# A decoder trunk on one core: the opening written out as one list per engine, Silu from Exp and Ln in the gated mixer, heads closed singly, 1/rms on VectorE

## The chip, the cores and the metric

The kernel runs on one core of a Trainium2 chip. The metric is the time of one execution on the device in microseconds (us), as the median of several runs. The engines are named as in the profile: PE is the matrix engine (TensorE) and PEld its weight loads, DVE is VectorE, ACT is ScalarE, POOL is GpSimd, SP is SyncE, whose queue issues most of the transfers. Each engine works through its own list of instructions in order and waits where an operand or a buffer is not ready.

## The reference

The program is a decoder trunk of two layers over 512 tokens of width 1024, all in 32-bit floats. Each layer is a half-step feed-forward block (FFN), a mixer, and a second half-step FFN, each behind an RMSNorm with a learned gain. Layer 0's mixer is gated linear attention (GLA) with 4 heads, layer 1's is stick-breaking attention (SB) with 16. Cut to what this change touches:

```python
def rmsnorm(x, g):
    y = x * lax.rsqrt(jnp.mean(x * x, axis=-1, keepdims=True) + EPS)
    return y * g

def swiglu(h, w_gate, w_up, w_down):          # width 2816 in between
    return (silu(h @ w_gate) * (h @ w_up)) @ w_down

# GLA, after the chunked attention has given o of 4 heads x 256:
    o = rmsnorm(o, o_norm)
    o = o * silu(g)                           # g: 1024 columns of h @ w_in
    return o @ w_out
```

## The kernel before

Activations are kept with features on the 128 partitions: `xs[0..7]` are eight tiles of 128 features by 512 tokens. Every large product is made three times to keep its precision: each operand is cut into a high part (cast on ACT, L133 for weights) and a low part (difference on DVE, L134), and `mm3` issues high x high, low weight x high and high weight x low.

Weights come through `feed`, a list of entries. An entry is a piece of a weight matrix with the products on it; a `feat` entry has eight steps over the input features with three products each, 24 products into one PSUM bank. Starting an entry cuts the weights of the next three and loads those of the next six. The weights' cuts have four buffers, so the cut of an entry waits until PE is done with the entry four before it. The order on each engine within these rules is found by a scheduler that works with costs of its own.

**Opening.** x arrives as eight tiles of 128 tokens by 512 features, four for the left half of the features and four for the right (L1288). PE turns them with transposes (`turn`, L1312), ACT and DVE make the cut `xh`, `xl` of x times the gain straight from PSUM (L1323, L1324), and the first two entries (gate and up weights of the first 128 columns, one transfer of 512 KB each) run on them. At this point 1/rms is not known. So the first entries of an FFN run on x that is not normed, and their results are multiplied by 1/rms on the way out of PSUM: the first two are held back (`defer`) until it is there, the next ones pay one more DVE operation each. Meanwhile `normed_input` makes the normed x (`xn`, L610), its cut `nh`, `nl` (L616, L617) and the sums `ts` that later entries need. `NORMED` = 6 is the entry from which the products run on `nh` and `nl`.

**1/rms.** `stats_a` sums the squares over features and calls `rstd`: a Sqrt on ACT (L384), with the table load that it needs, the reciprocal and a correction on DVE. `stats_b` spreads the four columns over 512 tokens with a product of ones and diagonal tiles (`dg`, `ps_R`) into `R` and `Rq`. This happens at the opening and once ahead of each of the five further blocks.

**GLA.** The feed's entries (queries, keys, values by `tok`, then the eight tiles of the gate g by `feat`, evacuated times R into `gn`, L754) are stepped between the levels of the four heads' attention, each of which has a chain DVE, ACT (Exp of `e`), DVE, PE (`ps_S`). `output(h)` normalizes a head: `vv` on DVE, Ln, Exp and Square on ACT, three DVE operations, then `on`. When the last head's levels are done, `silu` puts all eight `gn` through Silu (L966), the tables of Exp and Ln are loaded again (L434), and heads 0, 1 and 2 are closed: `on` times `gn` (L971), cut into `oh` (L974) and `ol` (L975). Then the output projection (`ps_b`, by `back`) begins, and head 3 is closed inside it.

Of the kernel before, what the change touches and what calls it, by code (L numbers as in the profile page):

```python
# [10 lines left out]
F32 = mybir.dt.float32  # L11
F32R = mybir.dt.float32r
BF16 = mybir.dt.bfloat16
U8 = mybir.dt.uint8
AF = mybir.ActivationFunctionType
# [15 lines left out]
def decoder(ctx: ExitStack, tc: tile.TileContext, a: dict, out: bass.AP):  # L31
# [345 lines left out]
    def rstd(sums, n, more=None):  # L377
# [5 lines left out]
        y = sp.tile([P, n], F32, tag="ry", bufs=2, name="ry")  # L383
        st["sqrt"] = nc.scalar.activation(y, v, AF.Sqrt).ins  # L384
        nc.vector.reciprocal(y, y)
        q = sp.tile([P, n], F32, tag="rq", bufs=2, name="rq")
        if n == 1:
            nc.vector.scalar_tensor_tensor(out=q, in0=y, scalar=v, in1=y, op0=ALU.mult, op1=ALU.mult)
        else:
            nc.vector.tensor_tensor(out=q, in0=y, in1=y, op=ALU.mult)  # L390
            nc.vector.tensor_tensor(out=q, in0=q, in1=v, op=ALU.mult)
        c = float(D) ** 0.5
# [49 lines left out]
    class FFN:  # L442
# [10 lines left out]
        def __init__(self, wg, wu, wd, gi, nxt, first=False, last=False):  # L453
            self.gi, self.normed = gi, False
# [3 lines left out]
            base, downs = len(feed.q), []  # L458
            self.sums_by = 10**6
            for group, (c0, c1) in enumerate(self.GROUPS):  # L460
                slots, put = 2 * (c1 - c0), 0
                for i in range(slots):
# [13 lines left out]
                    elif c not in self.SEVEN_UP:  # L476
                        feat(g, f_, self.evac_g, defer=d, part=3 if len(feed.q) == 0 else KD // 2, o=quads, m=four)
                    elif f == 0:
                        feat(g, 0, self.evac_g, o=quads, m=four), feat(g, 1, self.evac_g, o=quads, m=four)
# [194 lines left out]
        def run(self, between=None):  # L674
            with tc.tile_pool(name="hp", bufs=8, reuse_waits="tile") as self.hp, tc.tile_pool(
# [8 lines left out]
                for job, n in ((self.normed_input, self.NORMED - 2), (self.sums, self.sums_by - self.NORMED)):  # L684
# [16 lines left out]
    class GLA:  # L701
        def __init__(self, w_in, w_gk2, b_gk, og, w_out, nxt):
# [15 lines left out]
            for c in range(4):  # L718
# [33 lines left out]
        def evac_g(self, j, ps):  # L752
# [3 lines left out]
            )  # L756

# [205 lines left out]
        def silu(self):  # L963
            for j in range(KD):
                with tc.issue_after(st["last"]):
                    s = nc.scalar.activation(self.gn[j], self.gn[j], AF.Silu).ins  # L966
            exp_ln_tables(s)

# [9 lines left out]
        def run(self):  # L978
            with ExitStack() as es:
# [7 lines left out]
                new_norm()  # L987
                self.gate_weights()
# [6 lines left out]
                exp_ln_tables(st["sqrt"])  # L995
# [6 lines left out]
                for h in range(4):  # L1002
# [28 lines left out]
    class SB:  # L1031
# [139 lines left out]
        def run(self):  # L1171
            with ExitStack() as es:
# [10 lines left out]
                new_norm()  # L1183
                two_halves()
# [3 lines left out]
                exp_ln_tables(st["sqrt"])  # L1188
# [79 lines left out]
    with tc.tile_pool(name="ip", bufs=1) as ip:  # L1268

        gls = [ip.tile([P, P], F32, name=f"gl{n}") for n in range(2)]  # L1270
        for gl in gls:
            nc.vector.memset(gl, 0.0)
        x0 = {}
        lead = phases[0].lead
# [7 lines left out]

        gains(0, ("ffn1_norm",))
        gains(1, ("mix_norm", "ffn2_norm", "gla_o_norm"))
        for hf in range(2):
            for i in range(NT):
                x0[i, hf] = ip.tile([P, T], F32, name=f"x0_{i}_{hf}")
                nc.sync.dma_start(x0[i, hf], a["x"][0, i * P : (i + 1) * P, hf * T : (hf + 1) * T])  # L1288
            for c in lead[:1] if hf == 0 else lead[1:]:
                c.pool = ip  # L1290
                c.load()
        st["ss"] = None
# [123 lines left out]
```

## Time and profile before

| | |
|---|---|
| runs | 1831.14, 1831.64, 1832.43 us; median 1831.64 |
| profiled execution | 1831.4 us |
| its span, first to last instruction | 1829.6 us, granted clock 0.997 |
| busy PE / PEld / DVE / ACT / POOL | 1794.3 / 1643.0 / 1458.5 / 944.3 / 8.5 us |
| HBM | 175.17 MB read, 97 GB/s over the span |

A row of the profile gives the source line, engine, operation, output and inputs with their shapes. In the order of time it begins with the start and the length in us; a count (x4) says that several were merged. What stands in brackets is the idle time of the engine just before and what ended it. The rows of waits give the waiting instruction, what it waited for, and us in total, times, and the longest. Lengths of neighbouring instructions overlap, since an engine begins the next before the last has drained; how often one comes is read from the starts.

### The profile page before, as it was taken

The numbers are of one execution on the slowest core, as the hardware profiler recorded it, in microseconds if no ns is written. First come the engines' busy times: TensorE is split into PE (matmuls) and PEld (weight loads), VectorE is DVE, ScalarE is ACT, GpSimd is POOL, SyncE is SP. The second block draws the span as 40 slices with busy tenths as digits, with TensorE's granted clock in tenths as the row PEclk, the third lists the DMA queues.
The fourth block names the chain that finished last, engine by engine and source line by source line (L and its number), as shares of the span: only waits on it lengthen the run. The fifth ranks groups of instructions, "written<-read, shape, count | busy, mean of one in ns | idle before, by whom it ended". The sixth has DMA issues, their size and how long they took to land.

```text
span 1829.6 us, 28900 instructions
## 1 busy us (share of the span) xinstructions
PE 1794.3 (98%) x11790; PEld 1643.0 (90%) x11790; DVE 1458.5 (80%) x2317; ACT 944.3 (52%) x1459; POOL 8.5 (0%) x20
## 2 busy tenths in 40 slices
PE   7999999999989999999999999999999999999998
PEld 6899999889978899999989999999888788999997
DVE  5987878775776988887888888787887769888785
ACT  5444444543674644444454444345888844444444
POOL 0000000100000000000000000000000000000000
PEclk9999999999999999999999999999999999999999
DMA  5333332322112333333223333233212133333321
GB/s 162 116 104 104 104 119 90 115 70 70 61 55 71 119 121 111 110 107 103 92 92 127 104 113 115 96 94 101 73 58 70 51 111 115 104 105 104 117 92 69
DMA packets 177576, 179.09 MB, mean 98 GB/s; under 512 B 4066, under 2 KB 167956, under 8 KB 177444
## 3 DMA queue, kind: packets, MB, share of 16 engines
q1 hardware_dynamic: 176192, 175.13, 29.6%
q8 instruction: 92, 1.51, 0.3%
q0 software_dynamic: 576, 1.05, 0.2%
q10 hardware_dynamic: 676, 1.07, 0.2%
q14 instruction: 40, 0.33, 0.1%
HBM read 175.17 MB, written 2.10 MB: 97 GB/s over the span
## 4 chain that ended last, share of the span: by engine, by line
PE 85%; DVE 6%; ACT 4%; DMA 3%; issue 1%; SPq 1%; DVEq 0%; ACTq 0%
PE ps_d L62 23%; PE ps_f L62 15%; PE ps_w L530 14%; PE ps_z L530 9%; PE ps_q L530 9%; PE ps_t L62 4%; PE ps_b L62 3%; DVE wl L134 2%; PE ps_S L62 1%; DMA raw<-in_ffn_w_up_dram 1%; DMA raw<-in_ffn_w_gate_dram 1%; PE ps_bt L62 1%; ACT wh L133 1%; PE ps_oT L1158 1%; PE ps_z L1096 1%
## 5 line engine op out<-in xcount | busy, mean ns | idle before, releaser
L134 DVE TENSOR_TENSOR wl<-raw,wh 128x1024 fp32r<-128x1024 f32 x244 | 261.8, 1073 | 61.9 <-ACT wh L133 61.0
L133 ACT CAST wh<-raw 128x1024 fp32r<-128x1024 f32 x244 | 225.9, 928 | 131.3 <-PE ps_f L62 41.8
L62 PE MATMUL ps_d<-hh,wh 128*128 128x512 f32 x672 | 254.9, 379 | 0.0
L62 PE MATMUL ps_d<-hh,wl 128*128 128x512 f32 x672 | 254.7, 379 | 0.0
L62 PE MATMUL ps_d<-hl,wh 128*128 128x512 f32 x672 | 254.7, 379 | 0.0
L133 ACT CAST wh<-s 128x1024 fp32r<-128x1024 f32 x136 | 142.2, 1046 | 117.1 <-PE ps_q L530 84.1
L134 DVE TENSOR_TENSOR wl<-s,wh 128x1024 fp32r<-128x1024 f32 x136 | 166.1, 1221 | 26.3 <-ACT wh L133 24.9
L62 PE MATMUL ps_f<-xh,wh 128*128 128x512 f32 x448 | 176.6, 394 | 5.3 <-ACT wh L133 3.7
L308 DVE SCALAR_TENSOR_TENSOR x<-ps_d,x 128x512 f32<-128x512 f32 x184 | 125.2, 689 | 61.2 <-PE ps_d L62 61.0
L62 PE MATMUL ps_f<-xh,wl 128*128 128x512 f32 x448 | 171.6, 383 | 0.5 <-DVE wl L134 0.5
L62 PE MATMUL ps_f<-xl,wh 128*128 128x512 f32 x448 | 170.9, 382 | 0.0
L530 PE MATMUL ps_z<-th,wh 128*128 128x256 f32 x544 | 149.9, 276 | 2.4 <-DVE u L541 2.4
L133 ACT CAST wh<-rawd 128x1024 fp32r<-128x1024 f32 x84 | 87.9, 1047 | 121.9 <-PE ps_d L62 103.9
L530 PE MATMUL ps_w<-nh,wl 128*128 128x256 f32 x544 | 149.6, 275 | 0.0
L530 PE MATMUL ps_w<-nl,wh 128*128 128x256 f32 x544 | 149.6, 275 | 0.0
L530 PE MATMUL ps_z<-th,wl 128*128 128x256 f32 x544 | 149.6, 275 | 0.0
L530 PE MATMUL ps_z<-tl,wh 128*128 128x256 f32 x544 | 149.6, 275 | 0.0
L530 PE MATMUL ps_w<-nh,wh 128*128 128x256 f32 x544 | 149.5, 275 | 0.0
L62 PEld LDWEIGHTS ps_d<-hl,wh 128*128 128x128 f32 x672 | 127.0, 189 | 18.0
L62 PEld LDWEIGHTS ps_d<-hh,wl 128*128 128x128 f32 x672 | 127.2, 189 | 16.6
L62 PEld LDWEIGHTS ps_d<-hh,wh 128*128 128x128 f32 x672 | 127.2, 189 | 16.5
L134 DVE TENSOR_TENSOR wl<-rawd,wh 128x1024 fp32r<-128x1024 f32 x84 | 102.8, 1224 | 34.7 <-ACT wh L133 34.3
(260 smaller groups left out, 4719.8 us busy)
## 6 DMA issues: line engine op xcount, KB each, us to landing
raw<-in_ffn_w_gate_dram SPq DMA_DIRECT2D x43, 1024.0 KB, 5.2
raw<-in_ffn_w_up_dram SPq DMA_DIRECT2D x43, 1024.0 KB, 5.2
rawd<-in_ffn_w_down_dram SPq DMA_DIRECT2D x84, 512.0 KB, 3.4
raw<-in_gla_w_in_dram SPq DMA_DIRECT2D x12, 1024.0 KB, 5.2
raw<-in_sb_w_in_dram SPq DMA_DIRECT2D x16, 512.0 KB, 3.7
raw<-in_gla_w_out_dram SPq DMA_DIRECT2D x4, 1024.0 KB, 4.9
raw<-in_sb_w_in_dram SPq DMA_DIRECT2D x4, 1024.0 KB, 5.2
raw<-in_sb_w_out_dram SPq DMA_DIRECT2D x4, 1024.0 KB, 4.8
```

Source lines behind the costliest of these rows:

```text
L62: st["pe"] = nc.tensor.matmul(ps, l, r, start=first, stop=last).ins
L133: nc.scalar.copy(h, r).ins,
L134: nc.vector.tensor_tensor(out=l, in0=r, in1=h.bitcast(F32), op=ALU.subtract).ins,
L308: nc.vector.scalar_tensor_tensor(out=x, in0=back_by(ps, 4), scalar=0.5, in1=x, op0=ALU.mult, op1=ALU.add)
L530: nc.tensor.matmul(pairs(o), l_, r_, start=first and j + n == 0, stop=j == 3 and n == 2, skip_group_check=True)
L1096: nc.tensor.matmul(o_, l_, r_, start=first, stop=last, skip_group_check=True)
L1158: nc.tensor.matmul(po[e * 64 : e * 64 + 64, j * P : T], self.v[j][:, c : c + 64], self.wt[p, e][bk][:, c0 : c0 + n], start=j == 0, stop=j ...
```

## The change

**The opening** is written out in one order (`manual_schedule`). PE begins with eight products of a tile of ones (`filler`, made by a memset on DVE) into a bank that nobody reads, and has eight more between the transposes. x's first half is turned tile by tile instead of feature block by feature block. The weights of the first two entries come in halves: the four steps for the left half of the features first, then x's right half, then the second four; they are also cut in halves (`w_high`, `w_low`). The eight products of the left half for both entries are interleaved with the transposes of x's right half. The gains other than the first are fetched from ACT's queue after its second square. The first FFN's third entry is also held back until 1/rms is known, and `NORMED` is 7 for this FFN.

**1/rms** (`rstd` for four columns): two DVE operations on the bits of v as integers give a first value, three rounds of three DVE operations refine it. ACT has no part in it. The four last ones at the end of the program (one column each) keep the Sqrt. **Tables:** those of Exp and Ln are loaded after the last Silu of the FFN ahead of a mixer instead of after the Sqrt.

**GLA:** `evac_g` makes Silu at once, as g times Exp(min(g, 0) - Ln(1 + Exp(-|g|))): Abs, Exp and Ln on ACT, one DVE operation, Exp on ACT, one DVE product. `silu` is gone. A head is closed when the next head's levels have been worked through (`self.close(h - 1)`). In the feed the two gate tiles of a head follow its value entry.

```diff
+        if n > 1:
+            nc.vector.tensor_scalar(
+                out=q.bitcast(I32), in0=v.bitcast(I32), scalar1=1, scalar2=None, op0=ALU.arith_shift_right
+            )
+            nc.vector.tensor_scalar(
+                out=y.bitcast(I32), in0=q.bitcast(I32), scalar1=-1.0, scalar2=float(0x5F3759DF), op0=ALU.mult, op1=ALU.add
+            )
+            for k in (1.0, 1.0, c):
+                nc.vector.tensor_tensor(out=q, in0=y, in1=y, op=ALU.mult)
+                nc.vector.scalar_tensor_tensor(out=q, in0=q, scalar=-0.5 * k, in1=v, op0=ALU.mult, op1=ALU.mult)
+                nc.vector.scalar_tensor_tensor(out=y, in0=q, scalar=1.5 * k, in1=y, op0=ALU.add, op1=ALU.mult)
+            return y
...
+            if first:
+                self.NORMED = 7
...
+                        feat(g, f_, self.evac_g, defer=self.defer if first and i == 1 else d, o=quads, m=four)
...
-                two_halves(stats_a, 2 - (feed.pos == 1))
-                stats_b(turned=True)
-                flush(self.defer)
+                if self.first:
+                    with tc.manual_schedule():
+                        feed.entries(1)
+                        stats_b(turned=True)
+                        flush(self.defer)
...
             for c in range(4):
                 tok(w_in, 1024 + c * 256, lambda i, ps, c=c: self.evac_v(c, i, ps), "a")
-            for c in range(4):
                 ch = Chunk(cols(w_in, 2048 + c * 256, 256), KD, 256)
...
+            g = self.gn[j]
+            t = self.ep.tile([P, T], F32, tag="sg", bufs=2, name="sg")
+            nc.scalar.activation(t, g, AF.Abs)
+            act(t, t, AF.Exp, scale=-1.0)
+            act(t, t, AF.Ln, bias=1.0)
+            nc.vector.scalar_tensor_tensor(out=t, in0=g, scalar=0.0, in1=t, op0=ALU.min, op1=ALU.subtract)
+            act(t, t, AF.Exp)
+            nc.vector.tensor_tensor(out=g, in0=g, in1=t, op=ALU.mult)
...
-        def silu(self):
-            for j in range(KD):
-                with tc.issue_after(st["last"]):
-                    s = nc.scalar.activation(self.gn[j], self.gn[j], AF.Silu).ins
-            exp_ln_tables(s)
...
+                exp_ln_tables(st["silu"])
-                exp_ln_tables(st["sqrt"])
...
                         for _ in prev:
                             feed.step(1)
+                        self.close(h - 1)
                     prev = self.output(h)
-                    if h == 3:
-                        while feed.pos < self.end:
-                            feed.step(1)
-                        feed.finish()
-                        next(prev)
-                        self.silu()
-                        for g in range(3):
-                            self.close(g)
+                while feed.pos < self.end:
+                    feed.step(1)
+                feed.finish()
...
+        fill(8)
+        square(0, 0)
+        turn(0, 0, range(4))
+        ps = psum("ps_g", "t")
+        nc.tensor.transpose(ps[:, 0:P], gls[0], ident)
+        nc.vector.tensor_copy(gT[:, 0:16], ps[:, 0:16])
+        square(0, 1)
+        turn(0, 1, range(4))
+        fill(3)
+        gains(1, ("mix_norm", "ffn2_norm", "gla_o_norm"))
+        square(0, 2)
+        turn(0, 2, range(4))
+        fill(1)
+        turn(0, 3, range(4))
+        fill(4)
+        high(0), low(0)
+        w_high(0, 0), w_low(0, 0)
+        prod(0, 0)
+        px += [psum("ps_x", t) for t in "tt"]
+        turn(1, 0, (4, 5))
+        high(1), low(1)
+        prod(0, 1)
...
```

In the instructions, the opening changes on PE as follows. Before, from the last transpose of x's left half (`x_3_0`) to the first products (`ps_f`) of the first entry:

```order
L1312 MATMUL ps_x<-ident,x_3_0_105 128x128
L1318 MATMUL ps_g<-ident,gl_91 128x128
L62 MATMUL ps_f<-xh,wh 128x512
L62 MATMUL ps_f<-xh,wl 128x512
L62 MATMUL ps_f<-xl,wh 128x512
```

The same place in the changed kernel:

```order
L1342 MATMUL ps_x<-ident,x_3_0_107 128x128 x4
L63 LDWEIGHTS filler
L63 MATMUL ps_i<-filler 128x512
...
L63 MATMUL ps_f<-xh,wh 128x512
L63 MATMUL ps_f<-xh,wl 128x512
L63 MATMUL ps_f<-xl,wh 128x512
L1342 MATMUL ps_x<-ident,x_0_1_113 128x128 x2
L63 MATMUL ps_f<-xh,wh 128x512
```

The products of a feature block now stand between transposes of x's right half (`x_0_1`), and fillers stand where PE had nothing.

On DVE, from the sum of squares (`rv`) to 1/rms over the tokens (`R`) in the first FFN; `wl` are cuts of weights for later entries, `rq` and `r` the small steps of 1/rms. Before:

```order
L1367 COPY gT<-ps_g 128x34
L1369 TENSOR_TENSOR sums<-sums_123,sums_124 128x4
L380 TENSOR_SCALAR rv<-sums 128x4
L134 TENSOR_TENSOR wl<-raw_121,wh 128x1024
L385 RECIPROCAL ry<-ry 128x4
L134 TENSOR_TENSOR wl<-raw,wh 128x1024
L390 TENSOR_TENSOR rq<-ry 128x4
L134 TENSOR_TENSOR wl<-raw,wh 128x1024
L391 TENSOR_TENSOR rq<-rq,rv 128x4
...
L404 TENSOR_SCALAR dg<-ident,r_303 128x128 x4
L409 COPY R<-ps_R 128x512
```

In the changed kernel:

```order
L1433 COPY gT<-ps_g 128x34
...
L135 TENSOR_TENSOR wl<-raw_125,wh 128x1024
L381 TENSOR_SCALAR rv<-sums 128x4
L135 TENSOR_TENSOR wl<-raw,wh 128x1024
L389 TENSOR_SCALAR rq<-rv 128x4
L135 TENSOR_TENSOR wl<-raw,wh 128x1024
L392 TENSOR_SCALAR r_325<-rq 128x4
...
L397 SCALAR_TENSOR_TENSOR rq<-rq,rv 128x4
L135 TENSOR_TENSOR wl<-raw,wh 128x1024
L398 SCALAR_TENSOR_TENSOR r_325<-rq,r_325 128x4
L414 TENSOR_SCALAR dg<-ident,r_325 128x128 x4
L419 COPY R<-ps_R 128x512
```

A further cut (`wl`) has come in front of the last small step, and the copy of the gains `gT`, which needs a transpose that PE has behind all products of the first two entries, stands ahead of it all.

On ACT, at the end of GLA, where head 2 is finished (`y` are the steps of its norm, `osq` and `sh` its squares) and `oh` is what the output projection needs. Before:

```order
L439 ACT_TABLE_LOAD
L439 ACTIVATE y<-vv 128x512
L439 ACT_TABLE_LOAD
L439 ACTIVATE kd<-kd 128x384
L439 ACTIVATE y<-y 128x512
L966 ACT_TABLE_LOAD
L966 ACTIVATE gn<-gn 128x512
L950 ACTIVATE y_5358<-y 128x512
L966 ACTIVATE gn<-gn 128x512
L434 ACT_TABLE_LOAD
L974 CAST oh<-on 128x512 x4
```

In the changed kernel (`sg` are the steps of the gate's Silu):

```order
L449 ACTIVATE y<-vv 128x512
L779 ACTIVATE sg<-gn 128x512
L449 ACTIVATE y<-y 128x512
L449 ACTIVATE sg<-sg 128x512
L978 ACTIVATE y_5461<-y 128x512
L449 ACTIVATE sg<-sg 128x512
L449 ACTIVATE kd<-kd 128x384
L449 ACTIVATE sg<-sg 128x512
L134 CAST wh<-raw 128x1024
L932 COPY kt<-ps_kd 128x384
L996 CAST oh<-on 128x512 x2
```

The table loads are gone, the gate's four steps stand between those of the norm, and only head 2's two `oh` are left here; those of heads 0 and 1 stand earlier.

More of the change, by code (lines that the diff above doesn't have):

```diff
@@ L14 @@
 U8 = mybir.dt.uint8
+I32 = mybir.dt.int32
 AF = mybir.ActivationFunctionType
@@ L1281, in gains @@
                 row += r.shape[0]
+        filler = ip.tile([P, T], BF16, name="filler")
+        nc.vector.memset(filler, 1.0)
+        for gl in gls:
+            nc.vector.memset(gl, 0.0)
         gains(0, ("ffn1_norm",))
-        gains(1, ("mix_norm", "ffn2_norm", "gla_o_norm"))
[L1285 to L1291, printed above, removed]
@@ L1346, in decoder @@
-        with behind(turned[2]):
-            feed.q[0].split()
-        with behind(st["cut"]):
-            keep(pst, 0)
-        body = feed.q[0].body(feed.q[0].W)
-        next(body)
-        with tc.issue_after(st["pe"]):
-            pst = turn(1)
-        with behind(turned[5]):
-            feed.q[1].split()
-        with behind(turned[7]):
-            keep(pst, 1)
-            feed.start()
-        with behind(st["cut"]):
-            squares(0, (2, 3))
-            squares(1, range(NT))
@@ L1362, in decoder @@
-        for _ in body:
-            pass
-        ps = psum("ps_g")
-        with tc.issue_after(st["pe"]):
-            nc.tensor.transpose(ps[:, 0:P], gls[1], ident)
+        nc.scalar.preload_act_table_set("silu_and_others")
+        for hf in range(2):
+            rows_of(hf)
+            first_weights(hf)
+        for c in lead[2:]:
+            c.pool = ip
+        for en in feed.q[2:8]:
+            for u in en.units:
+                u[0].load()
+        W = []
+        for _ in range(2):
+            W.append(tuple(wp.tile([P, KD, P], F32R, tag="w" + t, bufs=4, name="w" + t) for t in "hl"))
@@ new lines, in decoder, with fill, turn @@
+        px = [psum("ps_x", t) for t in "aazz"]
+        pg, pu = psum("ps_f", "z"), None
+        idle = psum("ps_i", "o")
+        sums = [ip.tile([P, NT], F32, name=f"sums{hf}") for hf in range(2)]
+        nh, nl = [], []
+        def fill(n):
+            for _ in range(n):
+                mm(idle, filler[:, 0:P], filler, True, True)
+        def turn(hf, i, ks):
+            for k in ks:
+                nc.tensor.transpose(
+                    px[k][:, i * P : (i + 1) * P], x0[i, hf][:, (k % 4) * P : (k % 4 + 1) * P], ident
+                )
@@ new lines, in decoder @@
+        fill(1)
[8 more added lines that the diff above has]
+        prod(0, 1)
+        turn(1, 1, (4, 5))
+        high(2), low(2)
+        prod(0, 2)
+        turn(1, 2, (4, 5))
+        high(3), low(3)
+        w_high(1, 0), w_low(1, 0)
+        prod(0, 3)
+        pu = psum("ps_f", "o")
+        prod(1, 0)
+        turn(1, 3, (4, 5))
@@ new lines, in decoder @@
+        keep(0, 1, 2, 3)
+        prod(1, 1)
+        px += [psum("ps_x", t) for t in "aa"]
+        for i in range(NT):
+            turn(1, i, (6, 7))
+        prod(1, 2)
+        square(0, 3)
+        prod(1, 3)
+        w_high(0, 1), w_low(0, 1)
+        for k in range(4, KD):
+            high(k), low(k)
+            prod(0, k)
+        w_high(1, 1), w_low(1, 1)
+        for k in range(4, KD):
+            prod(1, k)
+        f1.defer += [(f1.evac_g_, pg), (f1.evac_u_, pu)]
+        feed.q[2].split()
@@ L1367, in decoder @@
+        for i in range(NT):
+            square(1, i)
+        ps = psum("ps_g", "z")
+        nc.tensor.transpose(ps[:, 0:P], gls[1], ident)
         nc.vector.tensor_copy(gT[:, 16:50], ps[:, 16:50])
+        keep(4, 5, 6, 7)
         st["sums"] = sp.tile([P, NT], F32, tag="rq", bufs=2, name="sums")
         nc.vector.tensor_tensor(out=st["sums"], in0=sums[0], in1=sums[1], op=ALU.add)
+        st["ss"], st["nh"], st["nl"] = None, nh, nl
+        stats_a()
+        turn_[0] = 3
+        feed.pos = 2
```

118 lines of the change are left out of this document (55 added, 63 removed).

## The prediction

> **What bounds the kernel now.** I read the first and fourth part of the page, then the waits of TensorE (PE), the busy times by stretch, and the order of time where PE stands idle.
>
> ```profile
> PE 1794.3 (98%) x11790; PEld 1643.0 (90%) x11790; DVE 1458.5 (80%) x2317; ACT 944.3 (52%) x1459; POOL 8.5 (0%) x20
> PE 85%; DVE 6%; ACT 4%; DMA 3%; issue 1%; SPq 1%; DVEq 0%; ACTq 0%
> ```
> ```profile
> PE ps_R L62 <- DVE dg L404: 1.9, 1, 1.9
> PE ps_f L62 <- DVE wl L134: 2.1, 2, 1.7
> PE ps_S L62 <- DVE e L844: 1.1, 1, 1.1
> ```
> ```profile
> 0.00:10.00 10.00, 4.64 (x17) 3.39 (x17) 0.43 (x4) 2.62 (x5) 0.70 (x6) 1.00 0.75 240
> 10.00:20.00 10.00, 5.98 (x22) 4.62 (x23) 5.22 (x9) 5.08 (x9) 0.00 (x0) 1.00 1.11 322
> 30.00:40.00 10.00, 8.06 (x34) 6.62 (x33) 7.99 (x18) 3.68 (x6) 0.00 (x0) 0.83 0.00 1
> 540.00:550.00 10.00, 5.72 (x20) 4.61 (x21) 8.07 (x13) 8.73 (x13) 0.00 (x0) 0.83 0.00 0
> ```
> PE is busy for 1794.3 of 1829.6 us and its products stay as they are, so the prize is 35.3 us of idle time and what a slow clock costs. The rows by stretch (length, busy time of PE, PEld, DVE, ACT and POOL, granted clock, DMA share, GB/s) put 9.4 us of the idle time into the first 20 us and 4.3 into 540 to 550. A clock of 0.83 over 10 us is 3.4 us at half speed, 1.7 us lost, in each of two stretches.
>
> **The opening.** Before, PE's rows in order of time, and then those of the engines that feed it:
>
> ```profile
> 6.65 3.03 PE L1312 MATMUL ps_x<-ident,x 128*128 128x128 f32 x13 [0.17 <-DMA x<-in_x_dram]
> 13.55 0.79 PE L62 MATMUL ps_f<-xh,wh 128*128 128x512 f32 x1 [3.65 <-ACT wh L133]
> ...
> 17.96 0.63 PE L62 MATMUL ps_f<-xl,wh 128*128 128x512 f32 x1
> 18.39 1.81 PE L1312 MATMUL ps_x<-ident,x 128*128 128x128 f32 x13
> ...
> 28.78 0.38 PE L62 MATMUL ps_f<-xl,wh 128*128 128x512 f32 x1
> 28.99 0.38 PE L62 MATMUL ps_f<-xh,wh 128*128 128x512 f32 x1
> ...
> 34.98 1.25 PE L62 MATMUL ps_R<-dg,gT 128*128 128x128 f32 x8 [1.94 <-DVE dg L404]
> ...
> 54.49 0.59 PE L62 MATMUL ps_f<-nh,wh 128*128 128x512 f32 x2
> ...
> 59.61 0.48 PE L62 MATMUL ps_f<-nl,wh 128*128 128x512 f32 x1 [0.25 <-DVE nl L617]
> ```
> ```profile
> 10.15 2.42 ACT L1323 ACTIVATE xh<-ps_x,gT 128x512 fp32r<-128x512 f32 x4 [4.49 <-DVE gT L1319]
> 10.87 2.73 DVE L1324 SCALAR_TENSOR_TENSOR xl<-ps_x,gT,xh 128x512 fp32r<-128x512 f32 x4 [0.76 <-ACT xh L1323]
> ...
> 12.44 1.06 ACT L133 CAST wh<-raw 128x1024 fp32r<-128x1024 f32 x1
> ```
> ```profile
> 33.97 0.16 DVE L391 TENSOR_TENSOR rq<-rq,rv 128x4 f32<-128x4 f32 x1
> 34.16 0.17 DVE L393 TENSOR_SCALAR rq<-rq 128x4 f32<-128x4 f32 x1
> ...
> 34.64 0.87 DVE L404 TENSOR_SCALAR dg<-ident,r 128x128 f32<-128x128 f32 x4
> 36.26 0.69 DVE L409 COPY R<-ps_R 128x512 f32<-128x512 f32 x1 [0.75 <-PE ps_R L62]
> ...
> 41.85 0.69 DVE L666 TENSOR_TENSOR t<-t 128x512 f32<-128x512 f32 x1 [1.32 <-ACT t L659]
> ...
> 58.87 1.30 DVE L617 TENSOR_TENSOR nl<-xn,nh 128x512 fp32r<-128x512 f32 x2
> ```
> A 128x512 product comes every 0.43 us on the slow clock (17.96 to 18.39) and every 0.215 on the full one (28.78 to 28.99); a transpose takes 0.233 (3.03/13) or 0.139 (1.81/13). Ahead of 28.99, where the third list entry starts, stand 32 transposes of x and the 48 products of two entries.
>
> *Front.* No fillers are in the trace, so I price them as products. Eight end at about 1.5 + 8 x 0.43 = 4.9 us (1.5: an estimate for the memset ahead); their gain is the clock, their cost that x's first tiles, there from about 4 us, are turned a little later. Then the sixteen transposes, the gains' one and four more fillers, partly slow, end near 9.2 (8.1 all fast, 10.6 all slow). A 128x512 `xh` is 0.6 us of ACT (2.42/4), `xl` 0.68 of DVE (2.73/4), a half-size weight cut 0.55 (half of 1.06) and 0.6. So the first product comes near 10.4, not at 13.55, waiting for one `xh` and half a cut instead of four and a whole. The bytes are there: 2.4 MB by 10 us (240 GB/s), then 322 GB/s, put the last x tile at 10.7 us, the second weight halves (3.15 MB) at 12.3. DVE paces PE (0.68 per `xl`) until about 13.8; the 39 products and 11 transposes that are left then (0.215 and 0.139 each, 9.9 us) bring the third entry to 23.7, against 28.99. That is 5.3 us sooner.
>
> *1/rms.* The six-row chain with a Sqrt and its table load on ACT becomes twelve small DVE operations. A shift on integers has no row; the 128x4 rows come 0.2 us apart and I take that (bounds 0.16 and 0.4 each). DVE is in order, and behind the copy of the gains, which waits for PE at 23.7, stand two x copies (1.2), a sum, four `wl` cuts of 1.13 and twelve small ones (2.4): `dg` at 32.3, `ps_R` at 32.8, `R` at 33.9. PE gets there at 23.7 + 37 x 0.215 = 31.7 and waits 1.1.
>
> *What is late next.* From `R`, DVE needs 23.2 us to the `nl` for which PE waits at 59.61 (36.26 to 58.87 plus 0.6). The changed kernel has two more evacuations of 0.6 in between, one `ts` of 0.33 less, and most of the 1.32 us wait for a Silu behind its table load gone: 23.2 again, so that `nl` is there at 57.1. But one more entry runs on products that are not normed yet, and by then PE is 24 products further, worth 5.2 us: 59.6 - 57.1 + 5.2 = 7.7 us. PE waits some 3 us there in two parts, and 1.94 us of waiting brought a slow clock in the stretch 30 to 40; I take off 1.2 of its 1.7. **Opening: -6.5** (bounds: -8.5 with a front at 23.0 and no slow clock; -2.7 with all transposes and the first products slow).
>
> [...]
>
> **The gated mixer's end.** Before:
>
> ```profile
> 539.87 0.55 PE L902 MATMUL ps_kd<-ident,kd 128*128 128x128 f32 x3 [0.33 <-DVE kd L892]
> 544.70 0.80 PE L62 MATMUL ps_b<-oh,wh 128*128 128x512 f32 x1 [4.28 <-ACT oh L974]
> ```
> ```profile
> 535.47 1.28 ACT L439 ACT_TABLE_LOAD   x1
> 536.76 0.63 ACT L439 ACTIVATE y<-vv 128x512 f32<-128x512 f32 x1
> 537.41 1.28 ACT L439 ACT_TABLE_LOAD   x1
> ...
> 539.76 1.28 ACT L966 ACT_TABLE_LOAD   x1
> ...
> 541.60 0.61 ACT L950 ACTIVATE y<-y 128x512 f32<-128x512 f32 x1
> ...
> 544.03 2.18 ACT L974 CAST oh<-on 128x512 fp32r<-128x512 f32 x4
> ```
> ```profile
> 534.18 0.69 DVE L943 TENSOR_SCALAR vv<-ps_on 128x512 f32<-128x512 f32 x1 [0.59 <-PE ps_on L62]
> ...
> 544.16 1.41 DVE L957 SCALAR_TENSOR_TENSOR on<-ps_o,gT,y 128x512 f32<-128x512 f32 x2
> ```
> ```profile
> L439 ACT ACT_TABLE_LOAD x8 | 10.3, 1283 | 0.7 <-DVE e L841 0.6
> L966 ACT ACT_TABLE_LOAD x7 | 9.0, 1283 | 0.1
> ```
> All `oh` wait behind the last Silu and its loads. Now heads 0 to 2 close one by one, so the first `ps_b` finds `oh` ready; head 2 alone is late. From the start of its `vv` I count by these rows: DVE and ACT alternate through `y`, its Exp and Square with three gate activations of 0.55 between (4.2 us), then `vv`, gate, `y`, gate, two `on`, one product (5.4), one cast (0.55): 10.1 us. PE has 25 + 16 products, three transposes and `ps_s` to run until it needs that `oh`: 9.6 us. It waits 0.5, and about as much again for `ol`. Gone are 4.28 and 0.33 us and 1.6 of slow clock; new is 1.0: -5.2. The 15 loads at L439 and L966 (19.3 us of ACT) go too, and with them most of the 1.1 at `ps_S`. Against that, each of eight gates adds two DVE operations (0.65 and 0.6) and four ACT ones for one; ACT has room (52% busy), DVE less, and I set new waits at 1.0, as much as is saved. **Mixer: -5.2** (bounds -7.7 and -2).
>
> **Elsewhere.** Of all `ps_R` only the opening's was waited for (one wait in the row above), so the other five 1/rms chains lie behind products. Twelve operations at 0.2 are 2.4 us, about what load, Sqrt and five rows cost: 0, bounds -2 and +1. If that cover goes, each delay reaches `nl` and PE one for one.
>
> **Sum.** -6.5 - 5.2 = -11.7. The span was 1829.6, the profiled execution 1831.4, the median 1831.64; from the median it is 1820.
>
> **Rivals.**
> [...]
> *Head 2's chain takes the place of the old wait.* Each `sg` and `wh` stands in ACT's queue ahead of `y`; two more in front than I count, and a slow clock after it, cost 1.1 + 1.7, and with the mixer's 1.1 not saved 3.9: 1824. For: 8.73 of 10 us of ACT busy at 540. Against: four loads, 5.1 us, leave that very stretch.
> [...]
> *Slower.* In ACT's queue Abs, Exp and Ln of a gate (3 x 0.6) stand ahead of a level's Exp, and a further Exp (0.6): 2.4 us per gate if every level's `ps_S` waits for them, 19.2 for eight, giving 1839. It decides from five gates fully on the path (11.7/2.4). Against: before, a Silu between two loads (3.2 us) stood in that queue again and again, and `ps_S` waited 1.1 us in all.
>
> **How the numbers follow.** Forecast 0.62, its own range 1817 to 1823; a front at 23.0 with no slow clock and no new waits, near 1815, 0.06; cold fillers 0.14; head 2's chain 0.10; both 0.04; slower 0.04. The range of 8 in 10 is 1813.5 to 1827: it leaves out part of the slow case, of the double one and of the bounds together. Faster by over 0.2% is 0.62 + 0.06 + 0.14 + 0.10 = 0.92, less 0.01 for spread; same 0.05; slower 0.04.
>
> **What would show it.** Third entry's first product near 23.7 us; `ps_R` near 32.8; PE idle some 3 us before an `nl` or `nh` near 57 and not before; no wait above 1.5 us at `ps_b`, and a granted clock of 1.00 where 540 to 550 was with no table load between the mixer's first Exp and its last. [...]

## The result and the profile after

The changed kernel takes 1815.3 us (median of six executions, 1814.2 to 1818.52) against 1831.85 us (six, 1831.14 to 1832.6): a ratio of 0.9912, 95% interval 0.9899 to 0.9925, 16.5 us less. The profiled execution took 1816.56 us and its span is 1814.8.

The first and fourth part of the page of the changed kernel:

```profile
PE 1794.2 (99%) x11806; PEld 1640.7 (90%) x11806; DVE 1473.1 (81%) x2373; ACT 926.2 (51%) x1455; POOL 8.5 (0%) x20
PE 85%; DVE 8%; ACT 4%; DMA 3%; issue 1%; DVEq 0%; ACTq 0%; SPq 0%
```

PE's busy time is the same to 0.1 us, although sixteen fillers are in it; the span is shorter by the idle time, 35.3 us before and 20.6 now. The head of the list of PE's waits in the kernel before (us in total, times, longest), and one further down:

```profile
PE ps_x L1312 <- DMA x<-in_x_dram: 5.1, 3, 4.1
PE ps_b L62 <- ACT oh L974: 4.3, 1, 4.3
PE ps_f L62 <- ACT wh L133: 3.7, 1, 3.7
PE ps_z L530 <- DVE u L541: 2.4, 3, 1.9
...
PE ps_f L62 <- DVE q L729: 1.6, 1, 1.6
```

The same list of the changed kernel:

```profile
PE ps_f L63 <- DVE x L243: 1.7, 1, 1.7
PE ps_f L63 <- DVE q L749: 1.6, 1, 1.6
PE ps_i L63 <- DVE filler L1313: 1.5, 1, 1.5
PE ps_f L63 <- ACT nh L630: 1.4, 1, 1.4
...
PE ps_f L63 <- DVE nl L631: 0.8, 2, 0.5
...
PE ps_R L63 <- DVE dg L414: 0.5, 1, 0.5
```

Of the waits of 5.1, 4.3 and 3.7 us at the head of the old list, 0.3 us for `oh` is left; the first on the new one, for x at L243, is new. The stretches that answer to those of before (length, then busy time of PE, PEld, DVE, ACT, POOL, granted clock, DMA share, GB/s):

```profile
0.00:10.00 10.00, 8.01 (x36) 4.44 (x37) 2.87 (x8) 6.02 (x12) 0.70 (x6) 1.00 0.78 247
10.00:20.00 10.00, 10.00 (x56) 8.74 (x54) 8.59 (x13) 9.18 (x20) 0.00 (x0) 1.00 1.07 309
30.00:40.00 10.00, 9.74 (x49) 8.70 (x50) 8.90 (x17) 4.48 (x7) 0.00 (x0) 1.00 0.58 186
...
360.00:370.00 10.00, 10.00 (x32) 6.75 (x32) 3.14 (x5) 5.21 (x9) 0.00 (x0) 0.84 0.00 0
530.00:540.00 10.00, 9.73 (x46) 7.97 (x45) 7.62 (x12) 4.29 (x8) 0.00 (x0) 1.00 0.32 107
```

In the first 20 us PE stands idle for 2.0 us instead of 9.4, 30 to 40 and the mixer's end run at the full clock, but a slow stretch has appeared after 360. Ahead of the clock's first change (4.73 us here, 18.85 in the kernel before) the trace has no record of it, and the view prints 1.00, although products come every 0.43 us there.

To see where the time came from I set the two traces side by side by PE's products: when has each kernel done the same amount of them? The lead of the changed one is worked out from all product rows, with one typical duration for each kind:

| place (time in the kernel before) | lead, us | what the waits there were |
|---|---|---|
| end of the second entry, 29 | 7.3 | front; 4.08, 0.88, 3.65 and 0.47 us idle before, 1.50 and 0.40 now |
| behind `ps_R`, 43 | 10.5 | 1.94 us and a slow clock before, 0.46 now |
| behind `nl`, 69 | 10.2 | 1.67 + 0.25 before, 1.36 + 0.52 + 0.27 now |
| 184 | 12.6 | 1.90 us at `ps_z` before, none now |
| behind q, 380 | 10.6 | 1.60 us in both; slow clock behind it only now |
| inside the mixer, 530 | 10.9 | 1.09 us at `ps_S` before, 0.16 and 0.18 at other places now |
| first `ps_b` done, 590 | 16.6 | 4.28 + 0.33 and a slow clock before, 0.26 now |
| second FFN's start, 635 | 15.2 | 1.14 before, 1.70 + 0.25 now |
| end | 14.7 | |

Two of these steps, +2.2 at 184 and -2.0 at 380, are taken below for chance, and they nearly cancel.

### The profile page after: what moved, and what is told of

Same layout as the page of the kernel before. It is cut to its first block, busy times and chain, and to the rows that moved or that the text cites. A ratio compares the mean times of both kernels' runs of the same rounds, so it can differ in the third digit from the quotient of the medians.

```text
span 1814.8 us, 28968 instructions
## 1 busy us (share of the span) xinstructions
PE 1794.2 (99%) x11806; PEld 1640.7 (90%) x11806; DVE 1473.1 (81%) x2373; ACT 926.2 (51%) x1455; POOL 8.5 (0%) x20
## 4 chain that ended last, share of the span: by engine, by line
PE 85%; DVE 8%; ACT 4%; DMA 3%; issue 1%; DVEq 0%; ACTq 0%; SPq 0%
PE ps_d L63 23%; PE ps_w L544 14%; PE ps_f L63 14%; PE ps_z L544 9%; PE ps_q L544 9%; PE ps_t L63 4%; PE ps_b L63 3%; DVE wl L135 2%; PE ps_S L63 1%; DMA raw<-in_ffn_w_up_dram 1%; PE ps_bt L63 1%; PE ps_oT L1176 1%; PE ps_z L1114 1%; DMA raw<-in_ffn_w_gate_dram 1%; ACT wh L134 1%
## 5 line engine op out<-in xcount | busy, mean ns | idle before, releaser
L134 ACT CAST wh<-raw 128x1024 fp32r<-128x1024 f32 (+1 forms) x242 | 223.8, 927 | 130.0 <-PE ps_f L63 43.4
L63 PEld LDWEIGHTS ps_d<-hh,wl 128*128 128x128 f32 x672 | 127.2, 189 | 16.5
L63 PEld LDWEIGHTS ps_d<-hh,wh 128*128 128x128 f32 x672 | 127.2, 189 | 16.5
```

Of the source, the lines that this page charges most:

```text
L63: st["pe"] = nc.tensor.matmul(ps, l, r, start=first, stop=last).ins
L134: nc.scalar.copy(h, r).ins,
```

## The experiments

The runs fall into three groups, each beside its own executions of the kernel before: medians 1832.53 (the parts apart, 1/rms, closing), 1832.93 (fillers, 1/rms sooner, products at q) and 1833.63 us (seventh entry, banks, all three). The changed kernel, run again in the second and third group, took 1817.17 and 1817.23 us, ratio 0.9916 (0.9902 to 0.9929) both times. So times are compared within a group, or by ratios.

### The parts apart

The opening alone: the kernel before with these parts of the diff, and everything else as it was.

```diff
+    with tc.tile_pool(name="ip", bufs=1) as ip, tc.manual_schedule():   # the opening's list
+            if first:
+                self.NORMED = 7
+                        feat(g, f_, self.evac_g, defer=self.defer if first and i == 1 else d, ...)
```

> The kernel before with the opening of the changed one alone (one list per engine, fillers, weight halves, third entry held back, NORMED 7); 1/rms by Sqrt on ScalarE and the mixer stay as they were. Counted by the same products in both traces, the changed kernel is 10.2 us ahead of the kernel before at 60 us, 12.6 ahead from 164 us on (the wait of 1.90 us at ps_z there is gone), 16.6 ahead behind the mixer and 14.7 at the end. Theory, the opening as measured: its gain is 10.2 us and does not hang on the rest, so about 1821.6 (from 1831.85), and 1819.4 if the wait at 164 us also went because of the opening. Rival, the size that I had forecast, 6.5 us, with the rest given by 1/rms on VectorE: 1825.3.

Everything but the opening: `rstd`, `evac_g` with Silu, `close(h - 1)`, the tables and the feed's order.

> The kernel before with everything but the opening: Silu from Exp and Ln in the mixer, heads closed singly, 1/rms on VectorE, the tables' loads moved. Theory: the mixer's end gives what the traces show between 508 and 565 us, 5.7 us (lead from 10.9 to 16.6), and the blocks behind it take back 1.9, so about 1828.0; the slow opening keeps its 28.99 for the third entry. The wait of 1.90 us at ps_z near 164 us came with a weight transfer that took 7.9 us where others took 5.3: if it is an accident of one execution it need not be there; if it is there again, it belongs to the old opening. Rival: the parts help one another (the lead at the mixer comes from the earlier start), then less than 2 us: 1830 or more.

The opening alone took 1823.23 us (ratio 0.9947, 0.9934 to 0.9961), 9.3 less than before; the rest alone 1825.68 (0.9961, 0.9949 to 0.9974), 6.9 less. Together 16.2, what the whole change gives. So nothing shows that the parts hang on one another (each of the two differences is known to some 2.5 us), and the opening is worth about what the ledger says (9.3, by its interval 7.1 to 12.1; there 10.2), not the 6.5 of the forecast. The waits of PE between 480 and 560 us show which part did what; with the opening alone:

```profile
PE ps_b L63 <- ACT oh L986: 4.3, 1, 4.3
PE ps_S L63 <- DVE e L856: 1.1, 1, 1.1
PE ps_kd L914 <- DVE kd L904: 0.3, 1, 0.3
```

and with the rest alone:

```profile
PE ps_b L63 <- ACT oh L985: 0.3, 1, 0.3
PE ps_s L63 <- ACT kt L921: 0.2, 1, 0.2
```

The mixer's part leaves 0.3 of the 4.3 us and takes the other two waits away, that at `ps_S` too. And the wait at 164 us was in neither run, the old opening or not. In the kernel before, VectorE waited there for a weight:

```profile
162.27 0.69 DVE L515 TENSOR_TENSOR s<-raw 128x512 f32<-128x512 f32 x1 [3.19 <-DMA raw<-in_ffn_w_gate_dram]
```

That transfer of 1 MB took 7.9 us from issue to landing; the median of 43 like it is 5.2. Waits at `ps_z` behind a wait of VectorE for a weight stand in every profile of this study, 0.2 to 2.7 us in all, most of them near the same places (109, 675, 1003 or 1577 us); one near 164 stands in none of the thirteen others. The first trace of the kernel before has 2.4, that of the changed kernel 0.2. I take the 2.2 us between them for chance; of the kernel before there is one profile alone.

### 1/rms

```diff
-        if n > 1:            # twelve VectorE operations
+        st["sqrt"] = nc.scalar.activation(y, v, AF.Sqrt).ins
...
-                exp_ln_tables(st["silu"])
+                exp_ln_tables(st["sqrt"])
```

> The changed kernel with 1/rms by Sqrt on ScalarE again, and the tables of Exp and Ln loaded behind that Sqrt. Theory, as forecast (a term of 0, bounds -2 and +1): twelve VectorE operations 0.2 us apart (26.77 to 28.35 in the opening) cost what table load, Sqrt and five operations did (365.49 to 368.31), so within 1.5 us of the changed kernel, 1814 to 1817. Rival: the load and the Sqrt stand in ScalarE's queue where it is full (the opening's chain, the mixer's start), the wait of 0.46 us at ps_R grows by the 1.3 of a load and a slow clock follows: 1818.5 or more.

1816.66 us, ratio 0.9915 (0.9901 to 0.9928), the changed kernel's own: within its interval the form of 1/rms is worth nothing. The opening shows why even a sooner `dg` gave nothing. VectorE in the run with Sqrt:

```profile
28.62 0.87 DVE L405 TENSOR_SCALAR dg<-ident,r 128x128 f32<-128x128 f32 x4
...
35.67 1.22 DVE L135 TENSOR_TENSOR wl<-raw,wh 128x1024 fp32r<-128x1024 f32 x1 [1.73 <-ACT wh L134]
```

`dg` begins 6.2 us after the third entry's first product (22.41), 8.2 after it in the changed kernel. But then VectorE, in order, stands 1.73 us before a cut of weights whose buffer PE still holds, and `nl` comes no sooner.

### Closing singly

```diff
-                        self.close(h - 1)
...
                 feed.finish()
+                next(prev)
+                for g in range(3):
+                    self.close(g)
```

> The changed kernel with heads 0 to 2 closed together behind the last head's levels, as before, but Silu still made at once from Exp and Ln. In the kernel before, the wait of 4.28 us at ps_b stood behind eight Silu and two table loads (1.28 each) and six casts. Theory: the Silu and its loads made the wait, closing singly adds little; the first products wait under 1 us and the time is within 1 us of the changed kernel, 1814.5 to 1816.5. Rival: the single closing is what takes the casts out of the way; with six casts of 0.55 and six differences of 0.6 in a row the wait at ps_b is 2 us or more and a slow clock of 1.7 follows: 1818.5 to 1820.

1818.14 us, ratio 0.9922 (0.991 to 0.9935) against 0.9912 and 0.9916: not told apart by the time. The trace tells more. No wait for `oh` is left, although the heads are closed together again, so the 4.28 us came from the eight Silu and the two table loads. (The feed's new order, in which the gate tiles follow their value entry, stands in this run as in the changed kernel and was not tried apart.) But the twelve cuts now stand before head 3's work, and that waits:

```profile
PE ps_kd L930 <- DVE kd L920: 0.7, 1, 0.7
PE ps_s L63 <- ACT kt L932: 0.6, 1, 0.6
```

There this run falls 1.8 us behind the changed kernel, counted from 530 us on, and 1.2 counted from 508. So of the mixer's 5.8 us, closing singly holds 1.2 to 1.8, Silu without its table the rest.

### The changed kernel again, and the clock

> The changed kernel once more, as the measure for the others on this chip. In its first profile TensorE's clock was halved for 3.41 us from 359.72, behind a wait of 1.60 us at ps_f for q; in the run with Sqrt the same wait of 1.60 us, at 360.86, was not followed by a slow stretch. The slow stretches of one trace begin whole multiples of 3.413 us after one another (before: 18.85, 35.91, 544.50). Theory: the clock is set per stretch of 3.413 us on a grid that does not start with the program, from how long TensorE stood idle in the stretch before; so this profile's waits are the same as in the first to 0.1 us, while the slow stretch at q may be there or not, and executions differ by its 1.7 to 2 us. Rival: the slow stretch follows from the length of a wait alone; then it is there behind every wait of 1.6 us, at q too.

> The changed kernel, as the measure for the three others on this chip: 1815.3 and 1817.2 us in the two groups of runs so far, against 1831.85 and 1832.93 of the kernel before. Theory of the stretches of 3.413 us: the time from which the clock is full differs from execution to execution (4.73 and 7.18 us in its two profiles) and with it the start of the third entry by about half of that. Rival: it is the same in all.

Both theories held, but the first leaves a middle open: where PE worked for 1.58 to 1.72 us of a stretch, that time does not decide alone. But for those at `ps_z` (0.2 to 1.3 us in all), the waits are the same to 0.2 us (at q 1.60 three times); the full clock began at 4.73, 7.18 and 5.11 us, the third entry at 21.57, 22.77 and 21.75; and of the three profiles only the first has a slow stretch at q. Divided at those multiples of 3.413 us, the traces show what lay ahead of a slow stretch. The changed kernel's first trace, the stretch with the wait at q and the next:

```profile
356.30:359.72 3.42, 1.71 (x11) 1.26 (x10) 2.66 (x7) 0.00 (x0) 0.00 (x0) 1.00 0.95 303
359.72:363.13 3.41, 3.41 (x10) 2.69 (x8) 1.44 (x3) 0.62 (x1) 0.00 (x0) 0.50 0.00 1
```

its second:

```profile
358.75:362.17 3.42, 1.82 (x13) 1.55 (x12) 2.66 (x5) 0.00 (x0) 0.00 (x0) 1.00 0.82 281
362.17:365.58 3.41, 3.41 (x14) 2.13 (x12) 0.73 (x2) 1.23 (x3) 0.00 (x0) 1.00 0.00 0
```

and the run with the rest alone, where PE waited 2.53 us in one piece ahead of `nl`:

```profile
50.28:53.69 3.41, 2.14 (x10) 1.53 (x9) 3.41 (x9) 2.14 (x5) 0.00 (x0) 1.00 0.00 0
53.69:57.11 3.42, 1.99 (x8) 1.43 (x8) 3.42 (x7) 2.41 (x4) 0.00 (x0) 1.00 0.23 41
57.11:60.52 3.41, 3.07 (x13) 2.40 (x14) 3.41 (x8) 1.90 (x5) 0.00 (x0) 1.00 0.77 266
```

The first number behind the length is PE's busy time. After 1.71 us of 3.41 the next stretch runs at 0.50, after 1.82 at 1.00; the 2.53 us of waiting are cut by a border into two parts that leave 2.14 and 1.99 busy, and nothing follows. Over the fourteen profiles of this study, a stretch at the full clock with at most 1.52 us of PE work was always followed by a slow one (six times ahead of the program's end: 0.00 and 1.47 us in the kernel before, 0.00 with the rest alone, 1.31 with the opening alone, 1.45 with `NORMED` at 6, 1.52 with the products at q), with 1.58 to 1.72 six times of ten (1.61, 1.65, 1.71 and 1.72 among those followed by one, 1.67 at 162.21 us in the kernel before among the others), with 1.80 or more never. So the length of a wait alone did not tell whether the clock was halved: 2.53 us left it full, and the same 1.60 us at q brought a slow stretch in four of the twelve profiles that have them. What the wait left busy of one stretch told more, and that depends on where the program happens to lie against the grid. The grid does not start with the program: its borders are whole multiples of 3.413 us apart, but the clock is full from 4.73 us on in one execution and from 7.18 in the next.

### The fillers

```diff
         def fill(n):
-            for _ in range(n):
-                mm(idle, filler[:, 0:P], filler, True, True)
+            return
```

> The changed kernel without its sixteen fillers. With them the clock was full from 4.73 us on. [...] Rival: the transposes and the first products warm the clock about as early, and the opening waits for x and the weights anyway: within 1 us of the changed kernel.

1818.74 us against 1817.17 in the same group (ratios 0.9924, 0.9912 to 0.9937, and 0.9916): 1.6 us, more than the rival gave, and not surely told from nothing. The order of time says what the fillers do; without them:

```profile
5.06 2.97 PE L1341 MATMUL ps_x<-ident,x 128*128 128x128 f32 x12
8.67 0.79 PE L63 MATMUL ps_f<-xh,wh 128*128 128x512 f32 x1 [0.64 <-ACT wh L1361]
...
11.41 0.64 PE L63 MATMUL ps_f<-xh,wl 128*128 128x512 f32 x1
```

The transposes are slow (5.06 to 8.0) and the clock is full only from 12.81 on, yet the first product comes at 8.67, with fillers at 8.65: it waits for the weights' cut on ACT, not for PE. The loss is the half speed from 8.67 to 12.81, about 2 us, less a wait of 0.4; the third entry starts at 23.17. That is 0.4 to 1.7 us behind the starts in the eleven profiles with fillers (21.5 to 22.8).

### The seventh entry

```diff
-                self.NORMED = 7
+                self.NORMED = 6
```

> The changed kernel with NORMED at 6 as before: one entry fewer runs on products that are not normed. Theory: nl is bound by VectorE and comes when it came (54.69 for the first wait), one evacuation of 0.6 us sooner, but TensorE gets there 24 products sooner (5.2 us), so the waits in front of nh and nl grow from 2.1 to about 6.5 us, and one or two slow stretches (1.7 each) follow: 4.5 to 8 us slower than the changed kernel. This is the forecast's term of 5.2 us, taken away. Rival: VectorE, with TensorE's buffers free sooner and one operation less, has nl ready 3 us or more sooner: under 2 us slower.

1820.26 us against 1817.23 (0.9928, 0.9916 to 0.9941): 3.0 us, less than the theory and more than the rival gave. In its profile PE waits 1.96 and 1.55 us for `nh`, with two slow stretches behind, and falls 4.3 us back, 0.7 of it by a later front (22.30 for 21.57). TensorE's 5.2 us are not all lost, since `nh` is also there sooner (the first wait for it ends at 49.83 for 53.47); the entry is worth about 3. If the parts add up, that and the 1.6 of the fillers leave about half of the opening's 9.3 us to the halves of the weights, the order of the transposes and the third entry's holding back, which were not tried one by one.

### 1/rms sooner

The transpose of the gains moves from behind the last product of the second entry to ahead of the products of k = 4 to 7, and the cuts of weights that stood between the small steps of 1/rms move behind the diagonal tiles:

```diff
+        ps = psum("ps_g", "z")
+        nc.tensor.transpose(ps[:, 0:P], gls[1], ident)
         for k in range(4, KD):
...
-        ps = psum("ps_g", "z")
-        nc.tensor.transpose(ps[:, 0:P], gls[1], ident)
...
+        st["dgs"] = diagonals()
...
+                        if self in feed.q[3:7]:
+                            es.enter_context(tc.issue_after(st["dg_last"]))
                         nc.vector.tensor_tensor(out=l, in0=r, in1=h.bitcast(F32), op=ALU.subtract)
```

> The changed kernel with the opening's 1/rms sooner: the transpose of the gains stands four products earlier on TensorE (VectorE waited 2.71 us for it), and the four cuts of weights that stood inside the chain of twelve operations stand behind the diagonal tiles. Theory: VectorE is what the normed input waits for from 19 to 54 us; its 2.7 us of waiting at the gains' copy and the 0.72 at R go, nl is there about 3 us sooner, and the waits at 53.47, 54.69, 58.03 and 30.26 (2.6 us in all) go: 2 to 2.6 us less than the changed kernel. Rival: the postponed cuts come in the way later, or a cut that waits for its buffer blocks VectorE (in the run with Sqrt dg was there 1.2 us sooner and VectorE then waited 1.73 us for a cut whose buffer TensorE still held, so nothing was gained): within 0.5 us.

1814.77 us against 1817.17 (0.9899, 0.9884 to 0.9914): 2.4 us, though the two intervals overlap. `R` comes at 28.26 instead of 31.42, the wait at `ps_R` is gone, and of 2.15 us ahead of `nh` and `nl` this is left:

```profile
PE ps_f L63 <- DVE wl L137: 0.4, 1, 0.4
PE ps_f L63 <- ACT nh L637: 0.3, 1, 0.3
```

Measured against its own start, the run is 2.0 us ahead of the changed kernel at 60 us. The theory held: VectorE's chain sets the end of the opening, as long as nothing that waits for a buffer stands in it. Which of the two moves gave how much was not tried.

### More products at q

```diff
+                idle = psum("ps_i", "o")
+                for k in range(7):
+                    mm(idle, self.gs[:, k], st["h"][k], True, True)
                 flush(self.defer)
```

> The changed kernel with seven more products into a bank that nobody reads, in the 1.60 us in which TensorE waits for q at the mixer's start; 7 x 0.2155 is 1.5 us, so they lengthen nothing. Theory: TensorE no longer stands idle there, so no slow stretch follows in any execution; executions that had it get 1.7 to 2 us shorter, the others stay: the median is 0 to 2 us under the changed kernel's, and no granted clock below 1.00 between 350 and 370 us. Rival: the slow stretch there has another cause than the idle time, or the products delay those behind them: the stretch stays, or the time is 1.5 us longer.

1817.79 us against 1817.17 (0.992, 0.9906 to 0.9933): no gain. The wait for q is gone from the trace and no slow stretch follows, but none followed in the changed kernel's profile of this group either. This run had one after another wait instead, that for x at 578 us (1.52 us busy in its stretch, and a slow one behind). It settles nothing on the time.

### The banks

```diff
                 st["few"] = self.hp
+                if self.gi == 4:          # the second FFN
+                    turn_[0] += 1
```

> The changed kernel with one count added to the rotation of PSUM banks ahead of the second FFN. The opening written as a list takes 3 banks by rotation up to the first FFN as before (3 of 8), but that FFN then takes 108 where it took 109, so the second FFN begins with the last bank of the eight (one buffer, the one that the output projection's last tile is read from), not with the first. Theory: this is what makes the wait of 1.70 us at 579.14 (ps_f for x; 1.0 to 1.9 in every run with the new opening, absent with the old one): it goes, 1 to 1.7 us less, and a wait for ss at ps_st as before (1.14 us) may come back in part. Rival: the wait comes from the order on VectorE (evacuations one by one between the cuts instead of three in a row) and stays under another name: within 0.5 us.

In the changed kernel PE waits at the second FFN's start:

```profile
579.14 0.48 PE L63 MATMUL ps_f<-xh,wh 128*128 128x512 f32 x1 [1.70 <-DVE x L243]
```

With the other bank the waits between 560 and 625 us are these:

```profile
PE ps_f L63 <- DVE wl L135: 0.3, 1, 0.3
PE ps_f L63 <- ACT nh L630: 0.3, 1, 0.3
```

So the mechanism is shown, and the run gains 1.3 us there on the changed kernel. Its time does not show it: 1817.59 us against 1817.23 (0.9914, 0.9901 to 0.9928). The profiled execution gave it back at 55.80 us, where the waits for `nh` and `nl` left 1.65 us of a stretch busy and a slow one followed.

### All three edits

At the mixer's start, besides the two above:

```diff
-                self.gate_low()
+                self.gate_low(0, 5)
                 stats_b("t")
+                with tc.issue_after(st["R_mm"]):
+                    self.gate_low(5, KD)
```

and the cuts of the next two entries behind the diagonal tiles and behind q.

> The changed kernel with three edits together: the opening's 1/rms sooner (2.0 us by its profile), the bank rotation of the run above, and at the mixer's start the chain of twelve operations without the cut of weights that stood in it, with the last six of the sixteen low-rank gate products placed behind ps_R, so that TensorE has work while R and q are made. Theory: 2.0 us in the opening, 1.0 to 1.5 at the second FFN, 0.8 at the wait for q, whose slow stretch (1.7 in the executions that had it) cannot come: 4 to 5 us under the changed kernel's median. Rival: the mixer's postponed cuts hold up the gate's logits, and only the opening's 2.0 us are left.

1813.22 us (1812.9 to 1813.86) against 1817.23 (1815.97 to 1819.57): all its executions lie under all of the changed kernel's, 4.0 us less; 0.989 of the kernel before (0.9877 to 0.9904). What is left of the waits in question:

```profile
PE ps_f L63 <- DVE wl L139: 0.7, 2, 0.4
PE ps_f L63 <- ACT nh L640: 0.6, 2, 0.3
...
PE ps_f L63 <- DVE q L761: 0.5, 1, 0.5
```

## Why the prediction was right or wrong

The forecast was 1820.0 with its own range 1817 to 1823; 1815.3 lies under that range and inside the wide one (1813.5 to 1827). Its number is that of the case that had 0.06 (a front near 23, no slow clock, no new waits), but the way there is another: the front came sooner still, the opening's 10.2 us lie beyond the bound of 8.5 that I had set for it, and a wait of 1.70 us that I had not looked for takes some of that back.

**The front: mis-sized by 2.1 us.** The changed kernel's PE rows:

```profile
1.50 3.48 PE L63 MATMUL ps_i<-filler 128*128 128x512 bf16 x8 [1.50 <-DVE filler L1313]
4.81 0.60 PE L1342 MATMUL ps_x<-ident,x 128*128 128x128 f32 x4
...
8.65 0.48 PE L63 MATMUL ps_f<-xh,wh 128*128 128x512 f32 x1
9.53 0.48 PE L63 MATMUL ps_f<-xh,wl 128*128 128x512 f32 x1 [0.40 <-DVE wl L1366]
...
21.57 0.46 PE L63 MATMUL ps_f<-xh,wh 128*128 128x512 f32 x1
```

The eight fillers end where I put them (4.8 for 4.9) and the clock is full from 4.73 us on, so the case of cold fillers (0.14), in which it stays slow behind them, fell, and with it that of both (0.04). But a transpose then comes every 0.11 us (4.81 to 5.25 for four), not every 0.139 to 0.233. The 0.139 was misread: the row at 18.39 lies across the border at 18.85, and behind it the kernel before has the same 0.11 (twelve in 1.47 us, with 0.27 for the last one alone):

```profile
18.95 1.47 PE L1312 MATMUL ps_x<-ident,x 128*128 128x128 f32 x12
```

The sixteen are through at 7.5, not at 9.2, and the first product comes at 8.65, not at 10.4. Then `xl` at 0.68 us each does not pace PE as I had it do until 13.8: after 9.53 there is no wait, since the transposes of the second half stand between the products. The third entry starts at 21.57 for 23.7, 7.4 us sooner than before.

Transposes alone raised the clock in one trace. In the kernel before, the stretch of the row at 6.65, 5.20 to 8.61 us, has only 2.43 us of work, and the clock stayed slow behind it. The run with the rest alone has a stretch that they fill:

```profile
5.90:9.32 3.42, 3.29 (x15) 2.85 (x14) 0.00 (x0) 0.00 (x0) 0.00 (x0) 1.00 0.92 283
9.32:12.73 3.41, 0.00 (x0) 0.00 (x0) 2.65 (x5) 3.20 (x5) 0.00 (x0) 1.00 1.11 340
12.73:16.15 3.42, 2.75 (x6) 1.88 (x7) 2.61 (x4) 1.13 (x3) 0.00 (x0) 0.50 1.16 294
```

Its clock's first change is at 9.32, to full, behind 3.29 us of transposes, and the fall at 12.73 comes behind an idle stretch.

**1/rms and `nl`: right but for that start.** VectorE:

```profile
29.82 0.87 DVE L414 TENSOR_SCALAR dg<-ident,r 128x128 f32<-128x128 f32 x4
31.42 0.69 DVE L419 COPY R<-ps_R 128x512 f32<-128x512 f32 x1 [0.72 <-PE ps_R L63]
...
53.95 0.68 DVE L631 TENSOR_TENSOR nl<-xn,nh 128x512 fp32r<-128x512 f32 x1
```

`dg` is 8.2 us behind the front (forecast 8.6), `R` at 31.42 for 33.9, and `nl` is there at 54.6, the 23.2 us behind `R` of the forecast. By its formula that is 59.6 - 54.6 + 5.2 = 10.2, the lead measured.

**The slow clock ahead of `nl`: 1.2 us not lost.** The waits were 2.15 us for 3, and they left 1.94 of 3.41 us busy. The run with the bank edit shows the term as I had it, with 1.65 busy. I had read a slow clock as the consequence of a wait's length; in these profiles the same wait of 1.60 us at q brought one four times of twelve, so the term has a chance, not a size.

**The mixer's end: right, 5.8 us for 5.2.** From `vv` (523.27) to head 2's first `oh`:

```profile
532.43 1.22 ACT L996 CAST oh<-on 128x512 fp32r<-128x512 f32 x2 [1.67 <-DVE on L993]
```

are 9.8 us with the first of the two casts (10.1 forecast); PE gets there 9.6 us after `vv` (9.6 forecast) and waits 0.27:

```profile
533.11 0.48 PE L63 MATMUL ps_b<-oh,wh 128*128 128x512 f32 x1 [0.27 <-ACT oh L996]
```

`ol` was in time, so 0.3 of new waits stand for 1.0. The wait of 1.1 at `ps_S` went, and the new ones inside the mixer that I had set against it are 0.16 and 0.18. No table load is left between the mixer's first Exp and its last: of 30 loads in the program six remain, and the rival of heads that wait for the gates' activations fell.

**Elsewhere, 0: right for 1/rms, but one wait was overlooked.** I looked only for the chains of 1/rms. That the first FFN takes one bank fewer, and that the second then begins on the bank read last, is in no row of the trace of before; it follows from the code. The lead falls by 1.4 us there, and the bank edit wins 1.3 of them back. The run with the rest alone, which keeps the old rotation, does not have it.

**The sum.** With what the traces show, 10.2 + 5.8 + 0.3 (inside the mixer) - 1.4 (second FFN) - 0.5 (scattered in the second layer) is 14.4 for the forecast's 11.7; medians say 15.7 to 16.5. So the forecast's number was nearer than its terms: the opening's term was 3.7 short, and the second FFN and the second layer took 1.9 back. That the two first traces differ by 14.8 is in part luck on both sides, the 2.2 and 2.0 above. What the rest of the difference between traces and medians is made of, slow stretches and late transfers in the executions without a profile, was not tried.

## What to carry to other kernels

Here a wait of 1.60 us of the matrix engine was followed by half a clock for 3.41 us in four profiles of twelve, and of three executions of the changed kernel in one: cost such a wait as a chance, and compare a trace with a second trace of the same kernel before explaining a difference of 2 us. Where an engine works in order, look for what stands in the middle of a chain and waits for somebody else's buffer; moving it behind the chain, with the gains' transpose moved forward, was worth more here (2.4 us) than another form of the chain's steps (nothing within the interval). When an edit changes how many buffers are taken from a rotation, the wait can appear in a part of the program that the edit does not touch.

## What the runs showed of the hardware that I had not expected

Between its first change and the program's end the halved clock lasted one stretch of 3.41 us (35.91 to 39.33 in the kernel before) or two (6.83: 50.59 to 57.42 with `NORMED` at 6), on a grid that held through the whole execution: in the kernel before, borders between full and half clock lie at 18.85, 35.91 and 544.50 us, 5 and 149 times 3.413 apart. What came next went with how much of the stretch before was busy: at most 1.52 us of 3.41 was always followed by a slow one, 1.80 or more never, 1.58 to 1.72 went both ways, and what sets these ten apart was not tried. On the way up the figures are higher: behind a slow stretch with 2.94 us of work or more (the run with 1/rms sooner, 1.03 to 4.44 us) the clock was full in all fourteen profiles, behind one with 2.77 or less (the run without fillers, 5.99 to 9.40) it never was.

With fillers the clock was full sooner, and from when on depended on that grid too: in the eleven profiles with fillers it is full from 4.44 to 7.18 us on (12.81 without), and the third entry starts between 21.5 and 22.8. In the profile with 7.18 only 2.26 us of their work fell into the first stretch (0.35 to 3.76); in the first trace 3.23 us fell into one (1.32 to 4.73).

A transpose of 128x128 in 32 bits came every 0.11 us on the full clock and every 0.213 on the half one, in the opening before (18.95 and 6.9 us) as in the new one (4.81 us in its first trace, 4.89 in its second).

Outside the opening, a few of the 1 MB transfers of the FFNs' weights take 6.5 to 8 us in each profile instead of 5.2, and PE waits up to 1.9 us behind one. Many of them recur near the same places (issued near 90, 585, 655, 985 or 1552 us in the changed kernel); the one of the longest wait, issued at 154 us in the kernel before, has no like in the others.
